# The down projection's loads in one fixed order in the SP queue

## The chip, the cores and the metric

The kernel runs on one core of one Trainium2 chip. A core has a matrix engine (PE), a vector engine (DVE), a scalar engine (ACT), a general engine (POOL), and SP, which here only issues transfers. Each runs its own instructions in order, and they wait for each other through semaphores. A transfer is issued by SP, ACT or POOL and moved by 16 DMA engines that all of them share. The metric is the device time of one execution in microseconds (us), as the median of several.

## What is computed

A decoder block on 1024 tokens of width 1024 in float32: a convolution branch and an mLSTM branch, merged, then a gated feed-forward layer, then a final norm. Only the last part matters here:

```python
h = rms_norm(x, norm_ffn_g[l]) * (1.0 + sc2) + sh2
gt, up = jnp.split(jnp.einsum("bsd,df->bsf", h, w_ffn_up[l]), 2, axis=-1)
x = x + g2 * jnp.einsum("bsf,fd->bsd", jax.nn.silu(gt) * up, w_ffn_down[l])
...
return rms_norm(x, final_norm_g)
```

The second product, with `w_ffn_down` (2816 x 1024), is the down projection.

## The kernel before

The down projection is done as a Strassen-like scheme. Activations, weights and output are cut into quadrants, and instead of eight products of quadrants there are seven steps, each a product of one activation combination (`act_d[0]` to `act_d[6]`, written to DRAM by the up projection) with one weight combination. A step has four **chains**, one for each 128 tokens, so there are 28 chains, numbered 0 to 27; chain n belongs to step n // 4, and chain 27 is done in two halves of 256 columns (`last`, L1422). A chain is `down_mm` (L1355): 11 blocks of 128 of the inner dimension with three matmuls each, since every float32 operand is split into a high half and a low half in the engine's rounded format (high by high, low by high, high by low). The first 128 x 512 result of each chain is evicted by `evict` (L1386) into the sums `U`, `V` or the residual rows `x1`.

Four kinds of loads feed this, all issued by SP:

- **Activations** `xr`, by `x_fetch(n)` (L1302): 128 x 1408 for one chain, into one of two buffers. `x_split` (L1337) lets ACT make the high half `xh` (L1339) and DVE the low half `xl` (L1340), of three buffers each. The load of chain n + 2 thus needs the split of chain n to be done.
- **Weights**, by `w_fetch(i, u)` (L1321): the weights of step i in six blocks u of two rows of 128 (the last of one). `WSTEP` says for each step whether a fresh quadrant goes into `reg[u]`, and whether a second one goes into an `other` tile (two buffers), from which DVE makes a difference in `reg[u]` (L1332, L1334). Then ACT and DVE split it into `wd` (L1207, L1208). Step 1 wants one fresh quadrant, steps 2 and 5 a fresh one and a second one, steps 3 and 4 a second one, step 6 a fresh one. `TURN` gives blocks 0 and 1, 2 and 3, 4 and 5 to the first three chains of the step before: they are formed then, and fetched one chain ahead of that.
- **Rows**: the residual tiles `x1`, by `load_x1` (L1379).
- **Broadcast rows** `g2row` (gate of the layer, L952) and `grow` (norm weights, L1454), read by the evictions.

The main loop (L1447) writes for each chain n: the activation load of chain n + 3, the broadcast rows or `x1` loads due, the split of chain n + 2, the forming of this chain's blocks, the fetch of the next blocks, the matmuls, the eviction. What an engine's queue holds in the end is decided by a scheduler, which picks among ready instructions by priority and by its own timeline. `queue_behind(ins, earlier)` (L180) ties an instruction behind another in the same queue; it adds no semaphore. Before the change one kind of load is tied so: each `x1` load behind the activation load of chain n + 3 of the same round (`fetched`). All others stand where the scheduler put them.

Of the kernel before, what the change touches and what calls it, by code (L numbers as in the profile page):

```python
# [16 lines left out]
D = 1024  # L17
# [29 lines left out]
UN = (2, 2, 2, 2, 2, 1)  # L47
# [8 lines left out]
def hybrid_block(ctx: ExitStack, tc: tile.TileContext, x, c, w_ada, b_ada, norm_mix_g, w_in, b_in,  # L56
                 conv_dw_w, conv_dw_b, conv_ln_g, conv_ln_b, w_conv_pw, b_conv_pw, qk_conv_w,
                 qk_conv_b, mlstm_norm_g, w_out, norm_ffn_g, w_ffn_up, w_ffn_down, final_norm_g, out):
    nc = tc.nc
# [120 lines left out]
    def queue_behind(ins, earlier):  # L180
        tc.add_manual_dep(ins.ins, earlier.ins.name,
                          mybir.DependencyInfo(mybir.DependencyClass.NoSync, mybir.DependencyReason.DATA),
                          reason="queue_behind")
# [13 lines left out]
    for i in range(4):  # L197
        t = pro.tile([128, 2, D], F32, name=f"xt{i}", tag=f"xt{i}")
# [40 lines left out]
    for q in range(2):  # L239
# [12 lines left out]
        for k in range(KT):  # L252
# [5 lines left out]
            ins = nc.scalar.activation(h, p, AF.Copy) if e == "s" else nc.vector.tensor_copy(h, p)  # L258
# [29 lines left out]
    def mod_products(g, acc):  # L288
        p = ps_a()
        out = [nc.tensor.matmul(p[:, i:i + 1], acc[:, i // 2, (i % 2) * 128:(i % 2) * 128 + 128], ones_col, start=True, stop=True)  # L290
               for i in range(4)]
        return p, out
# [34 lines left out]
    p, ins = mod_products(0, acc)  # L327
    for g in range(4):
# [37 lines left out]
        if g < 3:  # L366
            p, ins = mod_products(g + 1, acc)
# [574 lines left out]
    mrow_d = [dram.tile([8, 128], F32, name=f"mrow_d{i}") for i in range(2)]  # L942
# [6 lines left out]
        nc.sync.dma_start(mrow_d[i], mrow[:, i])  # L949

    def mod_row(i, t):
        nc.sync.dma_start(t, mrow_d[i].rearrange("(o k) d -> o (k d)", o=1).to_broadcast([128, D]))  # L952

    G2 = const.tile([128, KT], F32, name="G2")
    nc.vector.scalar_tensor_tensor(G2, sc2, 1.0, cols["ffn_g"], op0=OP.add, op1=OP.mult)
# [3 lines left out]
    x1_d = [dram.tile([128, D], F32, name=f"x1_d{i}") for i in range(8)]  # L959
    FP = FT // 2  # L960
    act_d = [dram.tile([128, FP, 512], F32, name=f"act_d{i}") for i in range(7)]
# [227 lines left out]

    wdq = wdn.rearrange("(j i p) e -> i p j e", i=2, p=128)  # L1190

    def w_load(t, quad, u):
        nc.sync.dma_start(t, wdq[quad // 2][:, 2 * u:2 * u + UN[u], quad % 2 * 512:quad % 2 * 512 + 512])

    def w_tiles(i, u):
        got = []
# [26 lines left out]
    ss0, ss1 = (up_.tile([128, 4, 4], F32, name=f"ss{i}") for i in range(2))  # L1223
    g1row = krow("g1row")
    mod_row(0, g1row)

    def banks(n):
# [71 lines left out]
    x1 = [fp.tile([128, D], F32, name=f"x1_{t}") for t in range(7)]  # L1299
    ss = fp.tile([128, 8, 4], F32, name="ssf")  # L1300

    def x_fetch(n):  # L1302
        raw = fp.tile([128, FP, 128], F32, name="xr", tag="xr", bufs=2)
        fetched[n] = nc.sync.dma_start(raw, act_d[n // 4][:, :, n % 4 * 128:n % 4 * 128 + 128])
        return raw

    fetched = {}

    raw_x = {n: x_fetch(n) for n in (1, 2)}
    x1.append(fp.tile([128, D], F32, name="x1_7"))  # L1310
    grow, g2row = (fp.tile([128, D], F32, name=n) for n in ("grow", "g2row"))
    reg = [fp.tile([128, UN[u], 512], F32, name=f"reg{u}") for u in range(NU)]
# [3 lines left out]
    def tok(half, t):  # L1316
        return t // 2 * 4 + half * 2 + t % 2

    other = {}

    def w_fetch(i, u):  # L1321
        fresh, second, _ = WSTEP[i]
        if fresh is not None:
            w_load(reg[u], fresh, u)
        if second is not None:
            other[u] = fp.tile([128, 2, 512], F32, name="other", tag="other", bufs=2)[:, 0:UN[u]]
            w_load(other[u], second, u)

    def w_form(i, u):
        sign = WSTEP[i][2]  # L1330
        if sign > 0:
            nc.vector.tensor_sub(reg[u], reg[u], other[u])  # L1332
        elif sign < 0:
            nc.vector.tensor_sub(reg[u], other[u], reg[u])  # L1334
        return w_split(i, u, reg[u])

    def x_split(raw):  # L1337
        hi, lo = (fp.tile([128, FP, 128], F32R, name=n, tag=n, bufs=3) for n in ("xh", "xl"))
        a = nc.scalar.activation(hi, raw, AF.Copy)  # L1339
        v = nc.vector.tensor_sub(lo, raw, hi.bitcast(F32))  # L1340
        turned.append((a, v))
        return [(hi[:, k, :], lo[:, k, :]) for k in range(FP)]
# [5 lines left out]
    def bank():  # L1348
        if not spares:
            m = [ps_mm(), ps_mm()]  # L1350
            spares.extend([m[1][:, 1], ps_n, m[0][:, 1], ps_c, m[1][:, 0], ps_a, m[0][:, 0], ps_c])
        t = spares.pop()
        return t() if callable(t) else t

    def down_mm(o, xp, wd, a, b):  # L1355
        for k in range(FP):
            (xh, xl), (wh, wl) = xp[k], [t[:, k % 2, a:b] for t in wd[k // 2]]
            nc.tensor.matmul(o, xh, wh, start=(k == 0), stop=False)  # L1358
            nc.tensor.matmul(o, xl, wh, start=False, stop=False)  # L1359
            nc.tensor.matmul(o, xh, wl, start=False, stop=(k == FP - 1))  # L1360
# [12 lines left out]
    def store(t, r):  # L1373
        nc.scalar.activation(x1[t], x1[t], AF.Copy, scale=r)
        nc.scalar.dma_start(out2[t * 128:(t + 1) * 128, :], x1[t])
# [1 line left out]
    LEFT, RIGHT = slice(0, 512), slice(512, 1024)  # L1377

    def load_x1(t, cs, n):  # L1379
        ins = nc.sync.dma_start(x1[t][:, cs], x1_d[t][:, cs])  # L1380
        queue_behind(ins, fetched[n])

    def both(x):
        nc.vector.scalar_tensor_tensor(ss[:, x, 2:3], ss[:, x, 0:1], EPS, ss[:, x, 1:2], op0=OP.add, op1=OP.add)  # L1384
# [1 line left out]
    def evict(i, t, p):  # L1386
        x = tok(i == 5, t)
        if i == 0:
            queue_behind(nc.scalar.activation(U[t], p, AF.Copy), turned[4 * i + t + 1][0])
        elif i == 1:  # L1390
            queue_behind(nc.vector.tensor_add(p, U[t], p), turned[4 * i + t + 1][1])
            residual(x, LEFT, p)
            square(x, LEFT, p, 0)
            nc.vector.tensor_mul(x1[x][:, LEFT], x1[x][:, LEFT], grow[:, LEFT])
        elif i == 2:
            queue_behind(nc.scalar.activation(V[t], p, AF.Copy), turned[4 * i + t + 1][0])
        elif i == 3:
            queue_behind(nc.vector.tensor_add(U[t], U[t], p), turned[4 * i + t + 1][1])
            nc.vector.tensor_add(V[t], V[t], U[t])
        elif i == 4:  # L1400
            queue_behind(nc.vector.tensor_sub(U[t], U[t], p), turned[4 * i + t + 1][1])
        elif i == 5:
            queue_behind(nc.vector.tensor_add(U[t], U[t], p), turned[4 * i + t + 1][1])
            nc.vector.tensor_add(p, V[t], p)
            residual(x, RIGHT, p)
            residual(x, LEFT, U[t])
            square(x, RIGHT, p, 1)
            square(x, LEFT, U[t], 0)
            both(x)
            nc.vector.tensor_mul(x1[x], x1[x], grow)  # L1410
            if t == 3:
                residual(tok(0, t), RIGHT, V[t])
            return x, rstd(x, 2)
        elif i == 6:
            queue_behind(nc.vector.tensor_add(p, V[t], p), turned[4 * i + t + 1][1])
            residual(x, RIGHT, p)
            square(x, RIGHT, p, 1)
            both(x)
            nc.vector.tensor_mul(x1[x][:, RIGHT], x1[x][:, RIGHT], grow[:, RIGHT])
            return x, rstd(x, 2)  # L1420
# [21 lines left out]
    for u in TURN[0]:  # L1442
        w_fetch(1, u)
# [3 lines left out]
    for n in range(N):  # L1447
        i, t = divmod(n, 4)
        if n + 3 < N:
            raw_x[n + 3] = x_fetch(n + 3)  # L1450
        if n == 1:
            mod_row(1, g2row)
        if n == 2:
            nc.sync.dma_start(grow, bass.AP(tensor=final_norm_g.tensor, offset=final_norm_g.offset, ap=[[0, 128], [1, D]]))  # L1454
        if 2 <= n < 6:
            load_x1(tok(0, n - 2), LEFT, n + 1)
        if 13 <= n < 17:
            load_x1(tok(1, n - 13), slice(0, D), n + 1)
        if 17 <= n < 21:
            load_x1(tok(0, n - 17), RIGHT, n + 1)  # L1460
        if n + 2 < N:
            splits[n + 2] = x_split(raw_x.pop(n + 2))
        if i < 6:
            for u in TURN[t]:
                nxt.append(w_form(i + 1, u))
        for u in TURN[(t + 1) % 4]:
            if i + 1 + (t == 3) < 7:
                w_fetch(i + 1 + (t == 3), u)
        xp = splits.pop(n)
        if n < N - 1:  # L1470
            p = bank()
            down_mm(p, xp, ready, 0, 512)
            for args in done_x:
                store(*args)
            out_x = evict(i, t, p)
            done_x = [out_x] if out_x else []
        else:
            for args in done_x:
                store(*args)
            last(t, xp, ready)  # L1480
        if t == 3:
            ready, nxt = nxt, []
# [29 lines left out]
```

## Time and profile before

| | us |
|---|---|
| median of 3 runs | 1716.25 |
| lowest and highest | 1715.08 and 1719.07 |
| the profiled execution's own time | 1714.31 |
| its span | 1712.6 |
| PE busy | 1666.8 |
| DVE busy | 1310.3 |
| ACT busy | 648.1 |

The span runs from the first to the last instruction, and its own time is 1.7 us longer. A busy matrix engine is not one at its peak, since matmuls are pipelined: one of 512 columns shows some 0.39 us, while the next starts 0.23 us after it. So the starts of matmuls tell more here than their durations.

### The profile page before, as it was taken

The page shows a single profiled execution, that of the slowest core. Times are in us where ns is not written, and L with a number is a line of the kernel's source. Part 1 is how long each engine was busy: PE and PEld are TensorE (multiplying, and loading weights), DVE is VectorE, ACT ScalarE, POOL GpSimd, SP SyncE. Part 2 cuts the span into 40 slices and gives each one's busy share as a digit, 9 for nine tenths or more (in the row PEclk, how much of TensorE's full clock was granted, in tenths as well). Part 3 has the DMA queues.
Part 4 walks back from the last instruction along what each step waited for, and adds up shares of the span by engine and source line. Part 5 has one row for each costly group of instructions (what it writes and reads, how often), then busy time and mean ns, then how long its engine had stood idle before and what let it go on. Part 6 is the DMA issues. An engine that isn't in the chain of part 4 may idle for free. (4 is left out here: it accounts for less than half of the span.)

```text
span 1712.6 us, 20833 instructions
## 1 busy us (share of the span) xinstructions
PE 1666.8 (97%) x8237; PEld 1394.1 (81%) x8237; DVE 1310.3 (77%) x1760; ACT 648.1 (38%) x835; POOL 59.5 (3%) x116
## 2 busy tenths in 40 slices
PE   5999999999999999999999999999999999989998
PEld 4798889888888889888888778888888888768887
DVE  6989998997699769638699577877677776659765
ACT  7425335322532253323611366422222222345343
POOL 0000001000001000000000000000000000000001
PEclk9999999999999999999999999999999999999999
DMA  9221111122112211234497644333223332598932
GB/s 324 64 63 50 38 62 38 50 63 73 38 46 65 62 49 39 74 106 140 145 381 248 204 141 143 110 105 105 93 92 105 105 113 103 181 304 256 333 119 103
DMA packets 221241, 211.12 MB, mean 123 GB/s; under 512 B 8455, under 2 KB 175127, under 8 KB 221143
## 3 DMA queue, kind: packets, MB, share of 16 engines
q1 hardware_dynamic: 202327, 164.70, 31.3%
q10 hardware_dynamic: 18576, 44.31, 6.8%
q8 instruction: 64, 1.05, 0.3%
q0 software_dynamic: 240, 0.79, 0.1%
q14 instruction: 34, 0.28, 0.1%
HBM read 168.60 MB, written 41.16 MB: 122 GB/s over the span
## 5 line engine op out<-in xcount | busy, mean ns | idle before, releaser
L395 DVE SCALAR_TENSOR_TENSOR cacc<-a,col,cacc 128x1024 f32<-128x1024 f32 x240 | 305.9, 1281 | 3.9 <-ACT cacc L393 1.4
L165 PE MATMUL mm<-hh,wlo 128*128 128x512 f32 x864 | 271.2, 391 | 1.6 <-DVE wlo L156 1.6
L165 PE MATMUL mm<-hl,whi 128*128 128x512 f32 x864 | 272.5, 392 | 0.0
L165 PE MATMUL mm<-hh,whi 128*128 128x512 f32 x864 | 271.6, 392 | 0.0
L165 PEld LDWEIGHTS mm<-hh,wlo 128*128 128x128 f32 x864 | 160.3, 188 | 33.7 <-DVE wlo L156 2.7
L165 PEld LDWEIGHTS mm<-hl,whi 128*128 128x128 f32 x864 | 161.0, 188 | 32.1 <-issue 0.5
L165 PEld LDWEIGHTS mm<-hh,whi 128*128 128x128 f32 x864 | 160.5, 188 | 31.6
L155 ACT ACTIVATE whi<-wraw 128x1024 fp32r<-128x1024 f32 x61 | 64.7, 1060 | 229.2 <-PE mm L165 182.1
L156 DVE TENSOR_TENSOR wlo<-wraw,whi 128x1024 fp32r<-128x1024 f32 x61 | 74.3, 1218 | 28.7 <-ACT whi L155 25.3
L1123 PE MATMUL mm<-Bh,gh 128*128 128x512 f32 (+1 forms) x192 | 71.5, 375 | 2.4 <-ACT mm L1020 1.3
L1124 PE MATMUL mm<-Bl,gh 128*128 128x512 f32 (+1 forms) x192 | 71.5, 373 | 0.6 <-DVE Bl L1042 0.6
L611 PE MATMUL mm<-wlo,hh 128*128 128x256 f32 x256 | 72.0, 282 | 0.0
L1125 PE MATMUL mm<-Bh,gl 128*128 128x512 f32 (+1 forms) x192 | 71.2, 371 | 0.0
L542 DVE SCALAR_TENSOR_TENSOR cacc<-qkraw,col,cacc 128x1024 f32<-128x1024 f32 x48 | 61.4, 1280 | 5.0 <-ACT cacc L540 4.5
L1358 PE MATMUL mm<-wd,xh 128*128 128x512 f32 (+1 forms) x154 | 60.4, 393 | 4.6 <-ACT xh L1339 4.6
L1359 PE MATMUL mm<-wd,xl 128*128 128x512 f32 (+1 forms) x154 | 60.4, 392 | 2.1 <-DVE xl L1340 2.1
L1339 ACT ACTIVATE xh<-xr 128x1408 fp32r<-128x1408 f32 x27 | 37.3, 1380 | 63.5 <-PE mm L1360 18.8
L1360 PE MATMUL mm<-wd,xh 128*128 128x512 f32 (+1 forms) x154 | 60.0, 390 | 0.0
L1340 DVE TENSOR_TENSOR xl<-xr,xh 128x1408 fp32r<-128x1408 f32 x27 | 43.7, 1620 | 17.8 <-ACT xh L1339 17.8
L610 PE MATMUL mm<-whi,hh 128*128 128x256 f32 x192 | 54.5, 284 | 0.0
L612 PE MATMUL mm<-whi,hl 128*128 128x256 f32 x192 | 54.2, 283 | 0.0
L611 PEld LDWEIGHTS mm<-wlo,hh 128*128 128x128 f32 x256 | 48.6, 190 | 0.0
(501 smaller groups left out, 3852.4 us busy)
## 6 DMA issues: line engine op xcount, KB each, us to landing
wraw<-in_w_in_dram SPq DMA_DIRECT2D x64, 512.0 KB
xr<-act_d SPq DMA_DIRECT2D x27, 704.0 KB
awt<-in_w_ada_dram SPq DMA_DIRECT2D x32, 512.0 KB
graw<-in_w_ffn_up_dram SPq DMA_DIRECT2D x24, 512.0 KB
act_d<-cg ACTq DMA_DIRECT2D x48, 256.0 KB
uraw<-in_w_ffn_up_dram SPq DMA_DIRECT2D x22, 512.0 KB
reg<-in_w_ffn_down_dram SPq DMA_DIRECT2D x20, 512.0 KB
other<-in_w_ffn_down_dram SPq DMA_DIRECT2D x20, 512.0 KB
```

What stands on the lines that cost most here:

```text
L155: nc.scalar.activation(hi, raw, AF.Copy)
L156: (eng or nc.vector).tensor_sub(lo, raw, hi.bitcast(F32))
L165: nc.tensor.matmul(flat(acc)[:, a:b], lhs[:, k, :], rhs[k][:, a:b], start=(first and k == 0), stop=(last and k == kt - 1))
L395: nc.vector.scalar_tensor_tensor(acc, a[:, j:j + S], dw_col(j, ct), acc, op0=OP.mult, op1=OP.add)
L542: nc.vector.scalar_tensor_tensor(cv, raw[:, j:j + S], wcol(j), cv, op0=OP.mult, op1=OP.add)
L611: nc.tensor.matmul(o[:, 0:256], hh[k][:, ts_], los[k], start=False, stop=False)
L1123: nc.tensor.matmul(o, a, rh, start=(k == 0), stop=False)
L1124: nc.tensor.matmul(o, a, rl, start=False, stop=False)
L1125: nc.tensor.matmul(o, b, rh, start=False, stop=(k == 3))
L1358: nc.tensor.matmul(o, xh, wh, start=(k == 0), stop=False)
L1359: nc.tensor.matmul(o, xl, wh, start=False, stop=False)
L1360: nc.tensor.matmul(o, xh, wl, start=False, stop=(k == FP - 1))
```

## The change

A list `in_line` collects the loads of this part as the program writes them, and `lined` ties each behind the one written before it: activations, weight blocks, `g2row`, `grow` and `x1`. The queue of SP then holds them in the order in which the loop writes them: for each chain the activations three chains ahead, then the broadcast row or `x1` tile due in that round, then that round's share of weight blocks. The `fetched` table falls away. Nothing else is edited.

```diff
@@ -949,7 +949,7 @@
         nc.sync.dma_start(mrow_d[i], mrow[:, i])
 
     def mod_row(i, t):
-        nc.sync.dma_start(t, mrow_d[i].rearrange("(o k) d -> o (k d)", o=1).to_broadcast([128, D]))
+        return nc.sync.dma_start(t, mrow_d[i].rearrange("(o k) d -> o (k d)", o=1).to_broadcast([128, D]))
 
     G2 = const.tile([128, KT], F32, name="G2")
     nc.vector.scalar_tensor_tensor(G2, sc2, 1.0, cols["ffn_g"], op0=OP.add, op1=OP.mult)
@@ -1189,8 +1189,16 @@
 
     wdq = wdn.rearrange("(j i p) e -> i p j e", i=2, p=128)
 
+    in_line = []
+
+    def lined(ins):
+        if in_line:
+            queue_behind(ins, in_line[-1])
+        in_line.append(ins)
+        return ins
+
     def w_load(t, quad, u):
-        nc.sync.dma_start(t, wdq[quad // 2][:, 2 * u:2 * u + UN[u], quad % 2 * 512:quad % 2 * 512 + 512])
+        return nc.sync.dma_start(t, wdq[quad // 2][:, 2 * u:2 * u + UN[u], quad % 2 * 512:quad % 2 * 512 + 512])
 
     def w_tiles(i, u):
         got = []
@@ -1301,10 +1309,9 @@
 
     def x_fetch(n):
         raw = fp.tile([128, FP, 128], F32, name="xr", tag="xr", bufs=2)
-        fetched[n] = nc.sync.dma_start(raw, act_d[n // 4][:, :, n % 4 * 128:n % 4 * 128 + 128])
+        lined(nc.sync.dma_start(raw, act_d[n // 4][:, :, n % 4 * 128:n % 4 * 128 + 128]))
         return raw
 
-    fetched = {}
 
     raw_x = {n: x_fetch(n) for n in (1, 2)}
     x1.append(fp.tile([128, D], F32, name="x1_7"))
@@ -1321,10 +1328,10 @@
     def w_fetch(i, u):
         fresh, second, _ = WSTEP[i]
         if fresh is not None:
-            w_load(reg[u], fresh, u)
+            lined(w_load(reg[u], fresh, u))
         if second is not None:
             other[u] = fp.tile([128, 2, 512], F32, name="other", tag="other", bufs=2)[:, 0:UN[u]]
-            w_load(other[u], second, u)
+            lined(w_load(other[u], second, u))
 
     def w_form(i, u):
         sign = WSTEP[i][2]
@@ -1377,8 +1384,7 @@
     LEFT, RIGHT = slice(0, 512), slice(512, 1024)
 
     def load_x1(t, cs, n):
-        ins = nc.sync.dma_start(x1[t][:, cs], x1_d[t][:, cs])
-        queue_behind(ins, fetched[n])
+        lined(nc.sync.dma_start(x1[t][:, cs], x1_d[t][:, cs]))
 
     def both(x):
         nc.vector.scalar_tensor_tensor(ss[:, x, 2:3], ss[:, x, 0:1], EPS, ss[:, x, 1:2], op0=OP.add, op1=OP.add)
@@ -1449,9 +1455,9 @@
         if n + 3 < N:
             raw_x[n + 3] = x_fetch(n + 3)
         if n == 1:
-            mod_row(1, g2row)
+            lined(mod_row(1, g2row))
         if n == 2:
-            nc.sync.dma_start(grow, bass.AP(tensor=final_norm_g.tensor, offset=final_norm_g.offset, ap=[[0, 128], [1, D]]))
+            lined(nc.sync.dma_start(grow, bass.AP(tensor=final_norm_g.tensor, offset=final_norm_g.offset, ap=[[0, 128], [1, D]])))
         if 2 <= n < 6:
             load_x1(tok(0, n - 2), LEFT, n + 1)
         if 13 <= n < 17:
```

SP, from the first weight block of step 1 on (`reg0` to `reg5` are its six blocks, `other` the second quadrant of step 2, `xr_11664`, `xr_11717` and `xr_11768` the activations of chains 3, 4 and 5, `x1_0` a row tile). Before:

```order
L1193 DMA reg0_11644<-in_w_ffn_down_dram 128x2x512
L1193 DMA reg1_11645<-in_w_ffn_down_dram 128x2x512
L1193 DMA reg2_11646<-in_w_ffn_down_dram 128x2x512
L1193 DMA reg3_11647<-in_w_ffn_down_dram 128x2x512
L952 DMA g2row_11643<-mrow_d1_7547 128x1024
L1193 DMA reg4_11648<-in_w_ffn_down_dram 128x2x512
L1193 DMA reg5_11649<-in_w_ffn_down_dram 128x512
L1454 DMA grow_11642<-in_final_norm_g_dram 128x1024
L1193 DMA other_11826<-in_w_ffn_down_dram 128x2x512
L1193 DMA other_11829<-in_w_ffn_down_dram 128x2x512
L1304 DMA xr_11664<-act_d0_7567 128x11x128
L1380 DMA x1_0_11629<-x1_d0_7559 128x512
```

and now:

```order
L1201 DMA reg0_11644<-in_w_ffn_down_dram 128x2x512
L1201 DMA reg1_11645<-in_w_ffn_down_dram 128x2x512
L1312 DMA xr_11664<-act_d0_7567 128x11x128
L1201 DMA reg2_11646<-in_w_ffn_down_dram 128x2x512
L1201 DMA reg3_11647<-in_w_ffn_down_dram 128x2x512
L1312 DMA xr_11717<-act_d1_7568 128x11x128
L952 DMA g2row_11643<-mrow_d1_7547 128x1024
L1201 DMA reg4_11648<-in_w_ffn_down_dram 128x2x512
L1201 DMA reg5_11649<-in_w_ffn_down_dram 128x512
L1312 DMA xr_11768<-act_d1_7568 128x11x128
L1460 DMA grow_11642<-in_final_norm_g_dram 128x1024
L1387 DMA x1_0_11629<-x1_d0_7559 128x512
```

The activations of chain 3 stood behind six blocks, two broadcast rows and two `other` blocks, and now stand behind two blocks; those of chains 4 and 5 moved ahead as well.

SP, some rows further (`xr_11818` and `xr_11865` are the activations of chains 6 and 7, and `reg0` and `reg1` are now the fresh blocks of step 2). Before:

```order
L1193 DMA reg0_11644<-in_w_ffn_down_dram 128x2x512
L1193 DMA reg1_11645<-in_w_ffn_down_dram 128x2x512
L1193 DMA reg2_11646<-in_w_ffn_down_dram 128x2x512
L1193 DMA reg3_11647<-in_w_ffn_down_dram 128x2x512
L1193 DMA reg4_11648<-in_w_ffn_down_dram 128x2x512
L1193 DMA reg5_11649<-in_w_ffn_down_dram 128x512
L1304 DMA xr_11768<-act_d1_7568 128x11x128
L1380 DMA x1_4_11633<-x1_d4_7563 128x512
L1304 DMA xr_11818<-act_d1_7568 128x11x128
```

and now:

```order
L1312 DMA xr_11818<-act_d1_7568 128x11x128
L1387 DMA x1_1_11630<-x1_d1_7560 128x512
L1201 DMA reg0_11644<-in_w_ffn_down_dram 128x2x512
L1201 DMA other_11826<-in_w_ffn_down_dram 128x2x512
L1201 DMA reg1_11645<-in_w_ffn_down_dram 128x2x512
L1201 DMA other_11829<-in_w_ffn_down_dram 128x2x512
L1312 DMA xr_11865<-act_d1_7568 128x11x128
L1387 DMA x1_4_11633<-x1_d4_7563 128x512
L1201 DMA reg2_11646<-in_w_ffn_down_dram 128x2x512
```

The fresh blocks of step 2 stood in one piece, with the first two `other` blocks far ahead of them; now each fresh block is followed by its `other` block, behind the activations of chain 6.

DVE, about the first differences of step 2 (`xl_11773`, `xl_11822` and `xl_11869` are the low halves of chains 4, 5 and 6; `wd_11777` and `wd_11780` the low halves of blocks 4 and 5 of step 1; `wd_11874` and `wd_11879` those of blocks 0 and 1 of step 2). Before:

```order
L1340 TENSOR_TENSOR xl_11773<-xr_11717,xh_11772 128x1408
L1332 TENSOR_TENSOR reg0_11644<-reg0_11644,other_11826 128x1024
L1332 TENSOR_TENSOR reg1_11645<-reg1_11645,other_11829 128x1024
L1208 TENSOR_TENSOR wd_11874<-reg0_11644,wd_11873 128x1024
L1208 TENSOR_TENSOR wd_11879<-reg1_11645,wd_11878 128x1024
L1340 TENSOR_TENSOR xl_11822<-xr_11768,xh_11821 128x1408
L1391 TENSOR_TENSOR pc_11888<-U0_11650,pc_11888 128x512
L1340 TENSOR_TENSOR xl_11869<-xr_11818,xh_11868 128x1408
```

and now:

```order
L1347 TENSOR_TENSOR xl_11773<-xr_11717,xh_11772 128x1408
L1216 TENSOR_TENSOR wd_11777<-reg4_11648,wd_11776 128x1024
L1216 TENSOR_TENSOR wd_11780<-reg5_11649,wd_11780 128x512
L1347 TENSOR_TENSOR xl_11822<-xr_11768,xh_11821 128x1408
L1339 TENSOR_TENSOR reg0_11644<-reg0_11644,other_11826 128x1024
L1216 TENSOR_TENSOR wd_11874<-reg0_11644,wd_11873 128x1024
L1339 TENSOR_TENSOR reg1_11645<-reg1_11645,other_11829 128x1024
L1347 TENSOR_TENSOR xl_11869<-xr_11818,xh_11868 128x1408
```

The two differences stood ahead of chain 5's low half, and now stand behind it and ahead of chain 6's, while the low halves of blocks 4 and 5 of step 1, which stood ahead of chain 3's, come between chain 4's and chain 5's. On PE the instructions stand in the same order as before.

## Rows read from the trace of the kernel before

**Rows 1.** The page of the profile: its first line (span and instructions of the profiled execution) and, of its part 1, the line of the matrix engine (busy us, share of the span, instructions).

```profile
span 1712.6 us, 20833 instructions
...
PE 1666.8 (97%) x8237; PEld 1394.1 (81%) x8237; DVE 1310.3 (77%) x1760; ACT 648.1 (38%) x835; POOL 59.5 (3%) x116
```

**Rows 2.** Busy time by stretch. Columns: stretch in us from the start of the span, its length, busy us and instructions of PE, of the weight loads, of DVE, ACT and POOL, then the granted TensorE clock as a share of full speed, the busy share of the DMA engines, and GB/s moved.

```profile
1490.00:1496.00 6.00, 6.00 (x26) 4.89 (x27) 3.90 (x3) 3.27 (x4) 0.00 (x0) 1.00 1.02 395
1496.00:1505.00 9.00, 9.00 (x40) 7.16 (x38) 4.27 (x4) 3.18 (x5) 0.00 (x0) 1.00 0.99 355
1505.00:1512.00 7.00, 1.56 (x4) 0.79 (x3) 1.62 (x1) 2.26 (x3) 0.00 (x0) 0.69 1.12 329
1512.00:1520.00 8.00, 8.00 (x31) 6.34 (x30) 6.26 (x5) 3.11 (x3) 0.00 (x0) 0.85 1.07 367
...
1528.00:1543.00 15.00, 15.00 (x66) 12.04 (x65) 14.73 (x16) 6.97 (x8) 0.00 (x0) 1.00 0.75 223
1543.00:1574.00 31.00, 31.00 (x134) 24.96 (x133) 29.77 (x31) 14.29 (x18) 0.00 (x0) 1.00 0.79 238
```

**Rows 3.** The timeline of PE in the down projection: start, duration, engine, line, operation with its operands, and in brackets the idle time before it and what ended that. Shown are the first two matmuls of chain 1, the first of chain 2, the first two of chain 3, the first of chains 4, 5 and 27, and the last matmul of all.

```profile
1488.19 0.45 PE L1358 MATMUL mm<-wd,xh 128*128 128x512 f32 x1
1489.89 0.50 PE L1359 MATMUL mm<-wd,xl 128*128 128x512 f32 x1 [1.25 <-DVE xl L1340]
...
1497.42 0.39 PE L1358 MATMUL pa<-wd,xh 128*128 128x512 f32 x1
...
1509.84 0.79 PE L1358 MATMUL mm<-wd,xh 128*128 128x512 f32 x1 [4.58 <-ACT xh L1339]
1511.50 0.79 PE L1359 MATMUL mm<-wd,xl 128*128 128x512 f32 x1 [0.87 <-DVE xl L1340]
...
1520.37 0.40 PE L1358 MATMUL pc<-wd,xh 128*128 128x512 f32 x1
...
1528.08 0.39 PE L1358 MATMUL mm<-wd,xh 128*128 128x512 f32 x1
...
1697.48 0.28 PE L1358 MATMUL mm<-wd,xh 128*128 128x256 f32 x1
...
1705.18 0.28 PE L1360 MATMUL pc<-wd,xh 128*128 128x256 f32 x1
```

**Rows 4.** The timeline of SP's queue of loads, merged by line: start of the first, time from there to the end of the last (waits between them included), line, and how many. L1193 is a block of weights, L952 the row g2row, L1304 the activations of a chain.

```profile
1483.47 2.35 SPq L1193 DMA_DIRECT2D reg<-in_w_ffn_down_dram  x4
1492.81 0.34 SPq L952 DMA_DIRECT2D g2row<-mrow_d  x1
1495.22 0.88 SPq L1193 DMA_DIRECT2D reg<-in_w_ffn_down_dram  x2
...
1496.63 2.74 SPq L1193 DMA_DIRECT2D other<-in_w_ffn_down_dram  x2
1499.48 0.53 SPq L1304 DMA_DIRECT2D xr<-act_d  x1
...
1507.33 3.26 SPq L1193 DMA_DIRECT2D reg<-in_w_ffn_down_dram  x6
```

**Rows 5.** The timeline of ACT: the high halves xh of chain 1's activations, of blocks 1, 2 and 3 of the weights of step 1 (wd), and the xh of chain 3, with the idle time before each.

```profile
1486.70 1.39 ACT L1339 ACTIVATE xh<-xr 128x1408 fp32r<-128x1408 f32 x1 [4.76 <-DVE cg L1159]
...
1491.43 1.06 ACT L1207 ACTIVATE wd<-reg 128x1024 fp32r<-128x1024 f32 x1 [0.22 <-DMA reg<-in_w_ffn_down_dram]
1494.99 1.06 ACT L1207 ACTIVATE wd<-reg 128x1024 fp32r<-128x1024 f32 x1 [2.51 <-DMA reg<-in_w_ffn_down_dram]
1496.93 1.06 ACT L1207 ACTIVATE wd<-reg 128x1024 fp32r<-128x1024 f32 x1 [0.88 <-DMA reg<-in_w_ffn_down_dram]
...
1508.41 1.38 ACT L1339 ACTIVATE xh<-xr 128x1408 fp32r<-128x1408 f32 x1 [4.96 <-DMA xr<-act_d]
```

**Rows 6.** The timeline of DVE: the low halves xl of chain 1 and of chain 3, and the first two differences of weights of step 2 (reg minus other), merged.

```profile
1488.21 1.62 DVE L1340 TENSOR_TENSOR xl<-xr,xh 128x1408 fp32r<-128x1408 f32 x1
...
1509.82 1.62 DVE L1340 TENSOR_TENSOR xl<-xr,xh 128x1408 fp32r<-128x1408 f32 x1 [5.50 <-ACT xh L1339]
...
1514.56 2.35 DVE L1332 TENSOR_TENSOR reg<-reg,other 128x1024 f32<-128x1024 f32 x2
```

**Rows 7.** The DMA issues of the last 273 us by what they load: issuing queue, how many, and KB of one (x is a row tile of the residual, x1).

```profile
xr<-act_d SPq DMA_DIRECT2D x27, 704.0 KB
reg<-in_w_ffn_down_dram SPq DMA_DIRECT2D x20, 512.0 KB
...
x<-x_d SPq DMA_DIRECT2D x8, 256.0 KB
...
reg<-in_w_ffn_down_dram SPq DMA_DIRECT2D x4, 256.0 KB
...
g2row<-mrow_d SPq DMA_DIRECT2D x1, 512.0 KB
grow<-in_final_norm_g_dram SPq DMA_DIRECT2D x1, 512.0 KB
```

**Rows 8.** What SP's queue waited for in the last 273 us: line that waited, who released it, us in total, times, longest.

```profile
SPq L1304 <- DVE xl L1340: 74.0, 21, 7.7
...
SPq L952 <- DMA act_d<-cg: 7.0, 1, 7.0
```

**Rows 9.** The timeline of POOL: two of its stores of activations.

```profile
1487.16 1.33 POOL L1168 DMA_DIRECT2D act_d<-cg  x2 [435.98 <-DVE cg L1182]
```

## The prediction

> **What bounds the kernel now.** The page comes first: the matrix engine (PE) is busy for 97% of the span [rows 1], so a load order can only win where PE stands. Next is the timeline of PE over the down projection, where a chain is 33 matmuls (11 blocks of the inner dimension, three products each). Chain 5 starts at 1528.08 and chain 27 at 1697.48, so 22 chains take 169.40, or 7.70 us each, with no idle time among them [rows 3]. Ahead of that two chains are longer. Chain 1 lasts from 1488.19 to 1497.42, 1.53 over 7.70; its second matmul waited 1.25 for DVE's low half xl. Chain 3 should start at 1497.42 + 7.70 = 1505.12. It starts at 1509.84, after 4.58 us without work that ACT's xh ended, and then waits 0.87 for xl. Chain 4 starts at 1520.37, where 1512.82 was possible [rows 3]. **So chain 3 costs 7.55 us:** 4.72 before it and 2.83 within it. Of the 2.83, 0.87 is the wait for xl, and the rest is a slower clock: after the pause the granted clock was 0.69 of full speed in 1505 to 1512 and 0.85 in 1512 to 1520, means between the levels of 1.2 and 2.4 GHz [rows 2].
>
> Why was xh late? ACT sat until 1508.41, when the activations of chain 3 landed [rows 5]. SP had issued that load at 1499.48, behind all six blocks of step 1, both broadcast rows and two "other" blocks of step 2 [rows 4], and from 1490 to 1520 the DMA was full at 329 to 395 GB/s [rows 2]. The two "other" blocks, issued at 1496.63, had their first use at 1514.56 [rows 4, 6]. Bytes wanted late went ahead of bytes wanted next.
>
> **The change, part by part.** It removes and adds no transfer and no arithmetic; every load keeps its size [rows 7]. PE's order of instructions is the same as before. The ordering itself adds no wait on a semaphore; it fixes who stands behind whom in SP's queue.
>
> *Chain 3's activations move ahead of blocks 2 to 5 and of everything behind them.* They need the buffer of chain 1's activations, free when xl of chain 1 ends: 1488.21 + 1.62 = 1489.83 [rows 6]. SP was past the four block loads by 1485.82 [rows 4], so it will stand there and issue at about 1489.9, 9.6 us earlier than now. The landing is bounded from both sides. In front: block 1 landed at 1491.43, block 2 at 1494.99, block 3 at 1496.93 [rows 5]; 704 KB in their place are block 2 and 192/512 of block 3's 1.94 us, so 1495.7. Behind: the present 8.93 us from issue to landing (1499.48 to 1508.41, with a fuller queue) give 1498.8. I take 1496, nearer the first, because only two blocks are still ahead. SP also stood 7.0 us at the g2row load until 1492.81, for a store of activations [rows 8]. If that wait should come ahead of the moved load, 2.9 us more make at most 1501.7. With 1.38 of xh and 1.62 of xl [rows 5, 6] the halves are ready at 1499.0 by the taken value and 1504.7 by the last bound, still before 1505.12. The whole stall goes: **minus 7.55**, and nothing below that from chain 1, since its xh stood on ACT behind earlier work until 1486.70 [rows 5], which does not move.
>
> *What is late next?* I walk the queue at 350 GB/s, from the 355 and 349 of the full stretches (1496 to 1505 has 355; 1505 to 1520 is 15 us with 329 and 367, mean 349 [rows 2]): 512 KB are 1.50 us, 704 KB 2.06, 256 KB 0.75. From 1496: blocks 2 and 3 at 1499.0, chain 4's activations 1501.1, g2row 1502.6, blocks 4 and 5 at 1504.8, chain 5's activations 1506.9, grow and a row tile 1509.1, chain 6's 1511.2, a row tile 1511.9. Chain 4 wants its activations split at 1512.82, chain 5 at 1520.52, chain 6 at 1528.22; each split takes 3.0. The covers are 8.7, 10.6 and 14.0 us. Block 5 of step 1 has until chain 4's last block at 1519.8. All of it hides behind chains 2 to 5.
>
> *The weights of step 2 move back.* Fresh and other blocks now alternate: 1513.4, 1514.9, 1516.4, 1517.9 for the first two pairs. On DVE the first two differences now stand ahead of chain 6's xl, so the second pair must land by 1528.22 - 1.62 - 1.2 = 1525.4 (a difference is 2.35 / 2 us [rows 6]): 7.5 us of cover. Of what follows, SP issues the third "other" load only when the first difference has freed its buffer; I count the bytes. From chain 4's activations and block 2 to the last pair they are 12,992 KB (13.30 MB: five activation loads, 1,792 KB of step 1, two broadcast rows, four row tiles, 5,632 KB of step 2), which takes 38.0 us, up to 1534.0. The last pair is wanted by chain 8's last block at 1543.62 + 7.0, less some 2.7 us of difference and split: 1547.9. The cover is 13.9 us, so nothing is paid. If the cover failed, each us beyond it is paid on PE.
>
> *Rows and later steps.* After chain 8 a step has 30.8 us per four chains; the activation loads wait for buffers that PE's own progress frees, and PE had no gap with the old order. g2row, grow and the first row tile land by 1509.1 in this walk and are read by the eviction of chain 4, which ends at 1520.5. Taken at zero; what covers them is that eviction's late place.
>
> A rule of the Trainium skill speaks against the move: "DMA: Bandwidth & Descriptors", Rules for kernel authors, says to issue a load early and wait for it late. The rows here differ on what that buys: the "other" loads were issued 17.9 us before their use, and PE paid for it at chain 3. By the rule the later step 2 loads should cost time; that is the first rival below.
>
> **The sum.** The profiled run took 1714.31 with a span of 1712.6 [rows 1]. 1714.31 - 7.55 = 1706.8. The median of before, 1716.25, lies 1.94 above the profiled run; from the median it is 1716.25 - 7.55 = **1708.7**.
>
> **Rivals.** *Partly given back.* SP in program order stands at each activation load until DVE has freed a buffer: 74.0 us in 21 such waits already [rows 8]. Weights behind it cannot pass any more. When SP was held by such waits the DMA ran at 238 GB/s (1543 to 1574) and 223 (1528 to 1543) [rows 2]. At 238 the 13.30 MB take 55.9 us, to 1551.9, and chain 8 stalls 4.0, with up to 2.0 more for the clock, as at chain 3. That returns 4.0 to 6.0: 1712.7 to 1714.7. For it: these rates. Against it: they come from stretches in which PE never waited, so SP had no reason to be faster, and the full stretches are those at issue. The Trainium skill states the mechanism ("DMA: Bandwidth & Descriptors", Anatomy of one DMA): the issuing sequencer waits on semaphores before it dispatches, not the DMA engines. The 74.0 us agree.
>
> *Slower.* The same place, further: the "other" tiles have two buffers, and each next load waits for a difference on DVE that stands behind evictions that wait for PE. If this paces the queue at 200 GB/s, a tenth below the lowest of those rows, the last pair lands at 1562.5: 14.6 late, 2.0 for the clock, 7.55 won, so 1725.3. It is slower by over 0.2% below 219 GB/s. Against it: the first two pairs need no such wait, and the last pair has 13.9 us of cover.
>
> *No change.* Chain 3's load is earlier in the queue, but lands no sooner, because the stores of the last activations, two by POOL at 1487.16 among them [rows 9], fill the DMA from 1490 to 1496 (395 GB/s [rows 2]) or because another operand is late for chain 3. For 1716.3 it would need 18.5 us from issue to landing, against 8.93 with a fuller queue.
>
> **How the numbers follow.** Full gain 0.72 at 1708.7; partly given back 0.11 around 1713.7; no change 0.09 at 1716.3; slower 0.08 at 1725.3. About 0.2% (3.4 us) is what a measurement here can tell from no change, so faster means below 1712.8. Of the second case a third is counted as faster and two thirds as the same: 0.76 faster, 0.16 same, 0.08 slower. The range takes the first case with the spread of the runs (1.2 below the median and 2.8 above it) and most of the second: 1706.5 to 1714.0. That leaves out some 0.2.
>
> **What would show it.** Right: chain 3's activations issued near 1490 and split by ACT at 1496 to 1499; chain 3 starting at about 1505.1 and chain 4 at 1512.8 with no idle time; a granted clock of 1.00 from 1505 to 1520; the last matmul near 1697.6 where it was 1705.18 [rows 3]; chain 1 still 1.5 too long. Wrong: an idle time of PE ahead of chain 6 or within chain 8, with SP standing at an activation load while weights wait behind it; or chain 3 still late, with its load issued after 1495.

## The result, and the profile after

The changed kernel takes 1707.35 us (median of 5 runs, 1706.31 to 1710.43), beside 1716.48 for the kernel before (median of 5, 1715.08 to 1719.53). The ratio of the means is 0.9944, with an interval from 0.9929 to 0.9959: 9.1 us are gone between the medians, 9.6 between the means, and by the interval 7.0 to 12.2. The forecast was 1708.7, from a gain of 7.55 on the 1716.25 of the three runs known then.

The profiled execution took 1706.31 us. These are the page's first line and its line of the engines' busy times, which answer to [rows 1]:

```profile
span 1704.6 us, 20805 instructions
...
PE 1664.8 (98%) x8237; PEld 1394.9 (82%) x8237; DVE 1310.5 (77%) x1760; ACT 647.5 (38%) x835; POOL 59.5 (3%) x116
```

The span is 8.0 shorter, PE's busy time 2.0 shorter. The rest is time in which PE stood. The timeline of PE says where (columns as in [rows 3]): the first two matmuls of chain 1, the first of chains 2 to 6 and of chain 27, and the last one.

```profile
1488.04 0.45 PE L1365 MATMUL mm<-wd,xh 128*128 128x512 f32 x1
1489.73 0.50 PE L1366 MATMUL mm<-wd,xl 128*128 128x512 f32 x1 [1.24 <-DVE xl L1347]
...
1497.27 0.39 PE L1365 MATMUL pa<-wd,xh 128*128 128x512 f32 x1
...
1504.94 0.39 PE L1365 MATMUL mm<-wd,xh 128*128 128x512 f32 x1
...
1512.61 0.40 PE L1365 MATMUL pc<-wd,xh 128*128 128x512 f32 x1
...
1520.27 0.40 PE L1365 MATMUL mm<-wd,xh 128*128 128x512 f32 x1
...
1527.94 0.39 PE L1365 MATMUL pn<-wd,xh 128*128 128x512 f32 x1
...
1688.98 0.28 PE L1365 MATMUL mm<-wd,xh 128*128 128x256 f32 x1
...
1696.69 0.28 PE L1367 MATMUL pc<-wd,xh 128*128 128x256 f32 x1
```

From chain 1 on there is one bracket, the 1.24 at the second matmul, as before. Chain 3 starts 7.67 after chain 2, chain 4 another 7.67 later; in [rows 3] they were 12.42 and 10.53 apart. The waits of PE from 1440 us on hold nothing else (engine, line, what released it, us in total, times, longest):

```profile
PE mm L1366 <- DVE xl L1347: 1.2, 1, 1.2
```

The timeline of SP's queue shows the cause (columns as in [rows 4]; L1312 is the activations, L1201 a weight block):

```profile
1483.32 1.33 SPq L1201 DMA_DIRECT2D reg<-in_w_ffn_down_dram  x2
1489.71 0.53 SPq L1312 DMA_DIRECT2D xr<-act_d  x1
1490.28 2.10 SPq L1201 DMA_DIRECT2D reg<-in_w_ffn_down_dram  x2
1492.78 0.87 SPq L1312 DMA_DIRECT2D xr<-act_d  x1
1493.70 3.04 SPq L952 DMA_DIRECT2D g2row<-mrow_d  x1
```

Chain 3's load is issued at 1489.71, the moment chain 1's xl (the first line of DVE below) frees its buffer, instead of at 1499.48 [rows 4]. ACT's timeline shows the high halves of chains 3, 4 and 5 made one after another as the loads land, and DVE's shows the xl of chains 1 and 3 and the first two differences of step 2 with chain 6's xl behind them:

```profile
1496.80 1.38 ACT L1346 ACTIVATE xh<-xr 128x1408 fp32r<-128x1408 f32 x1 [4.68 <-DMA xr<-act_d]
...
1502.81 1.38 ACT L1346 ACTIVATE xh<-xr 128x1408 fp32r<-128x1408 f32 x1 [0.90 <-DMA xr<-act_d]
...
1508.51 1.38 ACT L1346 ACTIVATE xh<-xr 128x1408 fp32r<-128x1408 f32 x1 [1.03 <-DMA xr<-act_d]
```

```profile
1488.06 1.62 DVE L1347 TENSOR_TENSOR xl<-xr,xh 128x1408 fp32r<-128x1408 f32 x1
...
1498.22 1.62 DVE L1347 TENSOR_TENSOR xl<-xr,xh 128x1408 fp32r<-128x1408 f32 x1 [4.19 <-ACT xh L1346]
...
1516.41 1.23 DVE L1339 TENSOR_TENSOR reg<-reg,other 128x1024 f32<-128x1024 f32 x1 [4.86 <-DMA other<-in_w_ffn_down_dram]
...
1519.97 1.22 DVE L1339 TENSOR_TENSOR reg<-reg,other 128x1024 f32<-128x1024 f32 x1
1521.11 1.62 DVE L1347 TENSOR_TENSOR xl<-xr,xh 128x1408 fp32r<-128x1408 f32 x1
```

ACT waits 4.68 for chain 3's activations, nearly the 4.96 of [rows 5], but now 11.6 us earlier, while PE still has chain 2 to do. A wait did not go away; it moved to where it costs nothing. Last the stretches (columns as in [rows 2]):

```profile
1505.00:1512.00 7.00, 7.00 (x32) 5.68 (x31) 4.30 (x4) 3.45 (x4) 0.00 (x0) 1.00 1.11 332
1512.00:1520.00 8.00, 8.00 (x36) 6.51 (x35) 2.40 (x3) 2.27 (x3) 0.00 (x0) 1.00 1.08 359
...
1543.00:1574.00 31.00, 31.00 (x135) 25.11 (x135) 22.05 (x23) 13.69 (x17) 0.00 (x0) 1.00 0.62 199
```

From 1505 to 1520 PE is busy throughout at a granted clock of 1.00, where it had 0.69 and 0.85, and the DMA moves as much as before: 332 and 359 GB/s beside 329 and 367. These are the same bytes in another order.

**Where the 8.00 us of span went**, from the starts in [rows 3] and above: chain 1 begins 0.15 earlier; from chain 1's start to chain 5's it is 32.23 where it was 39.89, 7.66; from chain 5's start to chain 27's 168.71 where it was 169.40, 0.69; and the end, from chain 27's start on, is 0.50 longer (15.62 and 15.12). This end takes 15.02 to 15.66 in the nine profiles below, 15.66 in one with the old stall (e2), so its 0.50 can't be put down to the change.

### The profile page after: what moved, and what is told of

The parts are those of the page before. It is cut to its first block, busy times and chain, and to the rows that moved or that the text cites. A ratio compares the mean times of both kernels' runs of the same rounds, so it can differ in the third digit from the quotient of the medians.

```text
span 1704.6 us, 20805 instructions
## 1 busy us (share of the span) xinstructions
PE 1664.8 (98%) x8237; PEld 1394.9 (82%) x8237; DVE 1310.5 (77%) x1760; ACT 647.5 (38%) x835; POOL 59.5 (3%) x116
## 5 line engine op out<-in xcount | busy, mean ns | idle before, releaser
L1215 ACT ACTIVATE wd<-reg 128x1024 fp32r<-128x1024 f32 (+1 forms) x36 | 35.2, 988 | 82.6 <-DVE reg L1339 54.2
L1216 DVE TENSOR_TENSOR wd<-reg,wd 128x1024 fp32r<-128x1024 f32 (+1 forms) x36 | 40.2, 1132 | 11.2 <-ACT wd L1215 11.0
```

## The experiments

Whole spans are a poor measure here, since the program ahead of the down projection, the same in every kernel, varies too: in the nine profiles chain 1 starts between 1488.04 and 1491.90. A lower clock goes with it. Of the stretches 250 to 300, 950 to 1000, 1000 to 1050 and 1050 to 1100 us, none has a mean granted clock below 1.00 in the profile of the change (chain 1 at 1488.04), one has 0.97 in before and in e3, e4 and e5 (1488.19 to 1489.92), two in e2, e6 and e7 (1488.89 to 1490.50), and three in e1 (1491.90); that the clock is the whole cause is not shown. So the table has, besides the medians, the time from chain 1's start to the end of the span in the one profiled execution of each. The first four experiments share their runs of the kernel before (median 1717.38), and so do the last three (1716.83), which ran on another chip; each ratio, again of means, is to the runs of before beside it.

| kernel | median, us | ratio to before, 95% | chain 1 to the end, us |
|---|---|---|---|
| before | 1716.48 | | 1712.6 - 1488.19 = 224.41 |
| the change | 1707.35 | 0.9944 (0.9929 to 0.9959) | 1704.6 - 1488.04 = 216.56 |
| e1_x3_first | 1709.65 | 0.9949 (0.9937 to 0.9962) | 1708.4 - 1491.90 = 216.50 |
| e2_x3_last | 1717.89 | 1.0002 (0.9993 to 1.0010) | 1713.8 - 1488.89 = 224.91 |
| e3_idle3 | 1708.24 | 0.9944 (0.9932 to 0.9957) | 1705.5 - 1489.57 = 215.93 |
| e4_idle8 | 1710.53 | 0.9963 (0.9950 to 0.9977) | 1709.0 - 1489.92 = 219.08 |
| e5_idle8_held | 1716.32 | 0.9994 (0.9985 to 1.0002) | 1715.3 - 1489.04 = 226.26 |
| e6_low_last | 1706.75 | 0.9938 (0.9924 to 0.9951) | 1705.0 - 1489.92 = 215.08 |
| e7_change_again | 1709.41 | 0.9954 (0.9942 to 0.9966) | 1708.6 - 1490.50 = 218.10 |

**Chain 3's load alone (e1_x3_first).** The kernel before, with one thing tied: the weight blocks and broadcast rows that the program writes after chain 3's activations stay behind them. The rest is left to the scheduler.

```diff
+    fetched = {}
+    def after_x3(ins):
+        if 3 in fetched:
+            queue_behind(ins, fetched[3])
+        return ins
...
-        nc.sync.dma_start(t, wdq[quad // 2][:, 2 * u:2 * u + UN[u], quad % 2 * 512:quad % 2 * 512 + 512])
+        ins = nc.sync.dma_start(t, wdq[quad // 2][:, 2 * u:2 * u + UN[u], quad % 2 * 512:quad % 2 * 512 + 512])
+        return after_x3(ins)
...
-            mod_row(1, g2row)
+            after_x3(mod_row(1, g2row))
...
```

> The kernel before, with one part of the change alone: every load written after chain 3's activations (blocks 2 to 5 of step 1, both broadcast rows, all later weights) is tied behind that one load; their order among themselves, and that of all other activations and rows, stays with the scheduler. Theory, that the gain is chain 3's stall and that this one load decides it: chain 3 starts near 1505 with no idle time before it, chain 4 near 1512.7, a clock of 1.00 throughout, and 1707 to 1709 us, as the whole change. Rival, that the fixed order of all loads is what gains: a PE wait at chain 3 or later remains and the time lies between 1711 and 1716.

It takes 1709.65, 0.65 above what I gave it and 1.35 below the rival's range, and its interval overlaps that of the whole change. From chain 1 on it needs 216.50, the change 216.56 (up to chain 27's start 201.33 and 200.94): the one load carries the gain. The timeline of PE, first matmuls of chains 2 to 5 and the second of chain 5:

```profile
1501.13 0.40 PE L1364 MATMUL pa<-wd,xh 128*128 128x512 f32 x1
...
1508.81 0.39 PE L1364 MATMUL mm<-wd,xh 128*128 128x512 f32 x1
...
1516.48 0.39 PE L1364 MATMUL pc<-wd,xh 128*128 128x512 f32 x1
...
1524.14 0.40 PE L1364 MATMUL mm<-wd,xh 128*128 128x512 f32 x1
1524.66 0.50 PE L1365 MATMUL mm<-wd,xl 128*128 128x512 f32 x1
```

Chains 2, 3 and 4 follow each other at 7.67. At chain 5 the second matmul comes 0.52 after the first instead of 0.23, and the chain takes 8.05. There the scheduler's order has no cover left: as in the kernel before, the first two differences of step 2 stand on DVE ahead of chain 5's xl, which DVE makes from 1522.98 to 1524.61, just ahead of that matmul. So the order of the other loads is worth about 0.4 us in this execution, and some cover.

**Chain 3's load last (e2_x3_last).** The change, with its fixed order, but with chain 3's activations behind blocks 2 to 5 of step 1, both broadcast rows and the first two "other" blocks.

```diff
...
+        if n == 0:
+            for u in (2, 3):
+                w_fetch(1, u)
+            lined(mod_row(1, g2row))
+            for u in (4, 5):
+                w_fetch(1, u)
+            lined(nc.sync.dma_start(grow, bass.AP(tensor=final_norm_g.tensor, offset=final_norm_g.offset, ap=[[0, 128], [1, D]])))
+            for u in (0, 1):
+                second(2, u)
         if n + 3 < N:
             raw_x[n + 3] = x_fetch(n + 3)
-        if n == 1:
-            lined(mod_row(1, g2row))
-        if n == 2:
-            lined(nc.sync.dma_start(grow, bass.AP(tensor=final_norm_g.tensor, offset=final_norm_g.offset, ap=[[0, 128], [1, D]])))
...
```

Here `second(2, u)` loads "other" block u of step 2; the blocks fetched here are left out further on.

> The change with one part undone: all loads in one fixed order, but chain 3's activations stand where they stood before, behind the six blocks of step 1, both broadcast rows and the first two other blocks of step 2. Theory: the load lands near 1508, chain 3 stands idle for 4 to 5 us and runs its first matmuls at a lower clock, and the time is 1714 to 1717 us, as before. Rival, that the order as a whole gains: no idle time above 1 us at chain 3 and 1707 to 1711 us.

The gain is gone: ratio 1.0002. The timeline of PE shows the two waits of [rows 3] again, at the same two matmuls of chain 3:

```profile
1511.16 0.80 PE L1367 MATMUL mm<-wd,xh 128*128 128x512 f32 x1 [5.24 <-ACT xh L1348]
...
1512.82 0.80 PE L1368 MATMUL mm<-wd,xl 128*128 128x512 f32 x1 [0.86 <-DVE xl L1349]
```

Behind them stands ACT, which waited 6.57 for the activations until 1509.73, as its timeline shows:

```profile
1509.73 1.38 ACT L1348 ACTIVATE xh<-xr 128x1408 fp32r<-128x1408 f32 x1 [6.57 <-DMA xr<-act_d]
```

The granted clock in 1505 to 1512 and 1512 to 1520 was 0.79 and 0.76. Idle time and median lie a little above what I gave them (4 to 5, and 1714 to 1717). This fixed order by itself gained nothing; the place of one load in it decides.

**The rival's mechanism, forced (e3_idle3, e4_idle8, e5_idle8_held).** Is there a point from which late weights of step 2 give the gain back? Idle transfers of 512 KB from DRAM to DRAM, which nothing reads, are put in the queue ahead of the first block of step 2: three, then eight.

```diff
+    idle_d = [dram.tile([128, 2, 512], F32, name=f"idle_d{j}") for j in range(3)]
...
+        if n == 3:
+            for j in range(3):
+                lined(nc.sync.dma_start(idle_d[j], wdq[0][:, 2 * (j % 5):2 * (j % 5) + 2, 0:512]))
```

> The change, plus three transfers of 512 KB from DRAM to DRAM that nobody reads, in line ahead of the blocks of step 2. By the walk at 350 GB/s each takes 1.5 us, 4.5 us in all; the trace of the change has chain 6's low half ready at 1522.7, and chain 6's second matmul at 1528.2, so 5.4 us of cover. Theory, that the move of step 2's weights is covered: no PE wait at chain 6, 1707 to 1708.5 us. Rival, that the queue in one order is paced by its waits and has little cover: a wait of 3 us or more at chain 6, 1711 us or more.

Three cost nothing (1708.24), and PE waits nowhere but at chain 1. But the cover was only half tested. The first difference of step 2 came 4.0 us later, counted from chain 1's start, and the scheduler had put chain 6's xl ahead of it.

The next kernel has 8 for 3 in the same lines.

> The change, plus eight such transfers in the same place: 12 us by the walk. Theory: the cover of 5.4 us is used up and 6 to 7 us appear as an idle time of PE at chain 6, with up to 2 us for a lower clock: 1713 to 1717 us. Rival, that these loads are covered anyway: no wait, 1709 us or less. If an idle transfer costs more than 1.5 us, the wait grows with it; its own duration is read from the queue.

It takes 1710.53, and from chain 1 to the end 2.5 more than the change: less than my theory asked for (1713 to 1717), more than its rival (1709 or less). DVE's timeline shows why, and PE's shows chain 7, its first two matmuls and chain 8's first:

```profile
1516.58 1.62 DVE L1348 TENSOR_TENSOR xl<-xr,xh 128x1408 fp32r<-128x1408 f32 x1 [2.66 <-ACT xh L1347]
1530.12 1.23 DVE L1340 TENSOR_TENSOR reg<-reg,other 128x1024 f32<-128x1024 f32 x1 [5.64 <-DMA other<-in_w_ffn_down_dram]
```

```profile
1537.47 0.40 PE L1366 MATMUL mm<-wd,xh 128*128 128x512 f32 x1
1539.48 0.50 PE L1367 MATMUL mm<-wd,xl 128*128 128x512 f32 x1 [1.62 <-DVE xl L1348]
...
1547.02 0.40 PE L1366 MATMUL pc<-wd,xh 128*128 128x512 f32 x1
```

The first difference is 11.8 us later than in the change, counted from chain 1 (eight transfers, so about 1.5 us each). But the scheduler had chain 6's xl made ahead of it, at 1516.58. Chain 7 paid most: its second matmul waited 1.62, and the chain took 9.55; chain 8's waited another 0.29. The theory's number rested on a DVE order that this kernel didn't have. To test it the order had to be held, so the next kernel, with the eight transfers as before, ties chain 6's xl behind the first two differences, as it stands in the change:

```diff
-            nc.vector.tensor_sub(reg[u], reg[u], other[u])
+            formed.append(nc.vector.tensor_sub(reg[u], reg[u], other[u]))
...
-        if n + 2 < N:
+        if n + 2 < N and n != 4:
             splits[n + 2] = x_split(raw_x.pop(n + 2))
...
+        if n == 4:
+            splits[6] = x_split(raw_x.pop(6))
+            queue_behind(turned[6][1], formed[1])
```

> As e4_idle8, with the order on DVE held as in the change: chain 6's low half behind the first two differences of step 2 (in e4_idle8 the scheduler had put it ahead of them, so that the wait appeared at chain 7 only). Theory, that this half covers 5.4 us in the change: the first other block lands some 12 us later than there, chain 6's low half is ready some 6 us too late, PE waits 5 to 7 us at chain 6 and runs on for a while at a lower clock: 1713 to 1717 us. Rival, that the late blocks themselves are what PE pays for, wherever the half stands: a wait of 2 to 3 us at chain 7 or 8 and 1709 to 1711.5 us, as in e4_idle8.

Now the same idle bytes cost all that the change had won: 1716.32, ratio 0.9994. The timelines of PE (first two matmuls of chain 6, first of chain 7) and of DVE:

```profile
1528.92 0.39 PE L1367 MATMUL pn<-wd,xh 128*128 128x512 f32 x1
1537.02 0.80 PE L1368 MATMUL pn<-wd,xl 128*128 128x512 f32 x1 [7.71 <-DVE xl L1348]
...
1546.12 0.39 PE L1367 MATMUL mm<-wd,xh 128*128 128x512 f32 x1
```

```profile
1530.72 1.22 DVE L1340 TENSOR_TENSOR reg<-reg,other 128x1024 f32<-128x1024 f32 x1 [7.12 <-DMA other<-in_w_ffn_down_dram]
...
1534.21 1.22 DVE L1340 TENSOR_TENSOR reg<-reg,other 128x1024 f32<-128x1024 f32 x1
1535.35 1.62 DVE L1348 TENSOR_TENSOR xl<-xr,xh 128x1408 fp32r<-128x1408 f32 x1
```

In the change chain 6's xl ends at 1521.11 + 1.62 = 1522.73 and the matmul that needs it would start about 0.23 after 1527.94: 5.4 us of cover. Here xl ends at 1536.97, counted from chain 1 13.2 later. 13.2 - 5.4 = 7.8, and PE waited 7.71, a little over the 5 to 7 that I gave. The chain took 1546.12 - 1528.92 = 17.20, 9.53 over 7.67: the other 1.8 goes with a granted clock of 0.81 from 1528 to 1537 and from 1537 to 1546. So late weights of step 2 can give the gain back. The wait grows us for us beyond the cover, the clock comes on top, and what carries it is the place of a late block's difference ahead of an xl in DVE's order. Two limits: the blocks were late here through idle transfers, not through waits of SP, and in e4 and e5 some matmuls of chains 8 to 10 also stand interleaved on PE, where e4 waits 0.29 and e5 nowhere.

**The wait that is left (e6_low_last), and the change once more (e7_change_again).** In chain 1 alone, the 11 matmuls with xl are done behind the 22 with xh.

```diff
...
+        if low_last:
+            for k in range(FP):
+                xh, (wh, wl) = xp[k][0], [t[:, k % 2, a:b] for t in wd[k // 2]]
+                nc.tensor.matmul(o, xh, wh, start=(k == 0), stop=False)
+                nc.tensor.matmul(o, xh, wl, start=False, stop=False)
+            for k in range(FP):
+                nc.tensor.matmul(o, xp[k][1], wd[k // 2][0][:, k % 2, a:b], start=False, stop=(k == FP - 1))
+            return
...
-            down_mm(p, xp, ready, 0, 512)
+            down_mm(p, xp, ready, 0, 512, low_last=(n == 1))
```

> The change, and in chain 1 alone the eleven matmuls with the low half xl moved behind the twenty-two with the high half xh. Chain 1 is the last chain that is too long: 9.23 us for 7.67, with PE waiting 1.2 for xl after its first matmul. Theory, that this wait is all of it: chain 1 takes 7.7 us, no PE wait above 0.3 us is left in the down projection, and the time is 1.5 us below the change run beside it: 1705 to 1707 us. Rival, that another operand is late there: chain 1 still takes 9 us or more.

> The change once more, on the same chip as the two others, so that they can be compared with it: 1706.3 to 1710.5 us, chains of the down projection at 7.66 to 7.71 us from chain 2 on, chain 3 without idle time.

e6 takes 1706.75 (1706.25 to 1707.16), e7 1709.41 (1709.27 to 1710.30): the two don't touch, and e6 is the fastest of this group. In e6 the waits of PE from 1440 us on are empty. The timeline of PE, chain 1's first matmul, its xl matmuls merged, and chain 2's first:

```profile
1489.92 0.46 PE L1366 MATMUL mm<-wd,xh 128*128 128x512 f32 x1
...
1495.09 2.73 PE L1369 MATMUL mm<-wd,xl 128*128 128x512 f32 x11
1497.66 0.39 PE L1373 MATMUL pa<-wd,xh 128*128 128x512 f32 x1
```

Chain 1 takes 7.74 where the change took 9.23, so this is worth 1.49 by the profile of the change. Beside e7 it is worth more, since that execution paid more at the same place, as its timeline of PE and its stretch from 1490 to 1496 show:

```profile
1490.50 0.49 PE L1365 MATMUL mm<-wd,xh 128*128 128x512 f32 x1 [0.37 <-ACT xh L1346]
1492.16 0.54 PE L1366 MATMUL mm<-wd,xl 128*128 128x512 f32 x1 [1.17 <-DVE xl L1347]
1492.50 0.63 PE L1367 MATMUL mm<-wd,xh 128*128 128x512 f32 x1
1492.92 0.63 PE L1365 MATMUL mm<-wd,xh 128*128 128x512 f32 x1
```

```profile
1490.00:1496.00 6.00, 4.46 (x12) 3.24 (x12) 5.48 (x5) 4.31 (x5) 0.80 (x2) 0.72 0.97 356
```

Matmuls are 0.43 apart instead of 0.23, and the granted clock has a mean of 0.72, between its two levels. Chain 1 took 10.75. Together 10.75 - 7.74 = 3.01 of the 3.6 us between the two profiled spans; the other 0.58 is that chain 1 began later.

## Why the prediction was right

- **The stall and its size.** The term was 7.55. From chain 2's start to chain 4's it is 15.34 where it was 22.95: 7.61, of which 0.06 is pace. e2 brings the stall back and e1 takes it away, each by the place of the one load.
- **Issue and landing.** Issue was put at about 1489.9 (measured 1489.71). Landing was put at 1496, between 1495.7 and 1498.8; ACT began at 1496.80. xl ended at 1499.84 where 1499.0 was expected, 5.1 us ahead of the start of chain 3. The g2row wait did not come first: g2row stands behind the moved load and the issues of the next ones, and no wait for the store that had held it 7.0 [rows 8] is left.
- **What is late next.** The walk at 350 GB/s put chain 4's and chain 5's landings at 1501.1 and 1506.9; ACT began on them at 1502.81 and 1508.51. The first difference of step 2 came at 1516.41 where the walk had its block at 1514.9. It is 1.5 to 1.7 too early throughout, and about 0.8 of that is already there at chain 3's landing. For the second pair I gave 7.5 of cover; what was left at chain 6 was 5.4. The last difference of step 2 began at 1537.48; the walk had its block at 1534.0, with a deadline of 1547.9. The signs and the order were right, the covers some 2 us too generous.
- **Partly given back, and slower.** Their mechanism can cost time (e5), but their condition did not arise. SP did stand longer at activation loads: 89.3 us in 22 waits, beside 74.0 in 21 [rows 8]. The bytes were not held up by it: from 1496 to 1537.5, up to the last difference of step 2, the DMA moved 337 GB/s, not the 238 or 200 of the rivals. It did run at 199 GB/s from 1543 to 1574, below the 219 from which I had the rival decide, and PE did not wait. So the mean rate of a later stretch was the wrong sign to decide by. The right quantity is when the block lands against when DVE's next xl is needed.

The waits of SP's queue, the line that answers to the first of [rows 8]:

```profile
SPq L1312 <- DVE xl L1347: 89.3, 22, 8.0
```

- **No change.** Excluded: from issue to landing chain 3's load took 1496.80 - 1489.71 = 7.1 us, not 18.5.
- **The sum.** 1706.8 was expected of the profiled execution, which took 1706.31. The median is 1.35 below 1708.7, inside the spread of single runs (1706.31 to 1710.43). Of the 9.1 between the medians 7.6 is the stall. No term of the sum covers the other 1.5, and no run shows its cause: in the two profiles pace gives 0.69 and the end takes 0.50 back, and chain 1's start differs by up to 3.9 between executions. The same program gained 7.4 between the medians in e7 (1716.83 and 1709.41). So the stall was sized rightly, and whether the median then lies 1.35 below or somewhat above the forecast is chance.

The Trainium skill, "DMA: Bandwidth & Descriptors", Anatomy of one DMA, has the issuing sequencer wait on semaphores before it dispatches. The section is on transfers from GpSimd, but the sentence speaks of the DMA engines as such, and the 89.3 us of waits on SP agree. Its Rules for kernel authors say to issue early and wait late. The measurements differ for a full DMA: in e2 (397 GB/s from 1490 to 1496) the "other" blocks are early again, ahead of chain 3's activations, and the kernel is as slow as before.

## What to carry to other kernels

When the DMA is full, as here at 329 to 395 GB/s, "early" is relative: a load issued long before its use is paid for by the one behind it in the queue, so sort the queue by when the consumer needs each load, and look for a first use many microseconds after the issue. Here the one load that PE waited for is nearly all of the gain; the fixed order of the others was worth 0.4 us at chain 5 (e1). Judge the cover of the others by landing time against need, on the engine that turns the data into operands and in that engine's order, not by the mean rate of a stretch.

## What the runs showed of the hardware that was not expected

- **A short wait can cost its clock too, or not.** The same program lost 9.23 - 7.67 = 1.56 us at chain 1 in one execution (wait 1.24, granted clock 1.00 from 1490 to 1496) and 10.75 - 7.67 = 3.08 in another (waits 0.37 and 1.17, then 0.72). In e2 waits of 0.25 and 1.17 at the same two matmuls left the clock at 1.00. Which one a run gets was not settled.
- **The steady pace has two values.** 33 matmuls take 7.67 us in the change and in e1, e2, e3, e6 and e7, and 7.70 in the kernel before from chain 4 on, in e5 from chain 7 on and in e4 from chain 11 on at the latest, at a granted clock of 1.00. A stall alone doesn't bring it (e2 has one and runs at 7.67). It makes 0.7 us between the two profiles here, and its cause is open.
- **Work ahead of the change varies more than many changes are worth:** chain 1 began anywhere in 3.9 us over nine profiles, and at 1488.04 and 1490.50 in two of the very same program.
